# One decode step in a two-layer hybrid decoder: four of the eight rows side by side in TensorE's column groups, without masks, and the second layer's step cut into five pieces between attention units

## The chip, the cores and the metric

The kernel runs on one core of a Trainium2 chip. The metric is the device time of one execution in microseconds (us); lower is better. The engines are named as the profile names them: PE (TensorE matmuls) and PEld (its weight loads), DVE (VectorE), ACT (ScalarE), POOL (GpSimd), SP (SyncE, which issues most of the DMAs).

## The reference, cut to what matters

A 1024-token prompt and eight decode rows (one token each) go through two layers together. Three places handle the eight rows by themselves, since each row has its own cache or state:

```python
def mem_attend(qm, mem_k, mem_v):            # both layers; 4 heads of 64, 256 memory tokens per row
    s = einsum('blhd,bmhd->bhlm', q, mem_k) * MEM_HEAD_DIM ** -0.5
    return einsum('bhlm,bmhd->blhd', softmax(s), mem_v)

def swa_sample(q, k_all, v_all, rel_bias, sinks):    # layer 1; 12 heads on 4 kv heads, 128 cached keys per row
    p = exp(s + bias - m);  p = p / (sum(p) + exp(sink - m));  return p @ v

def gla_chunk_step(S, inp):                  # layer 0; per row and head one 96 x 192 state
    S_new = exp(g) * S + k v^T;  o = q @ S_new
```

Everything else (norms, projections, MLPs, the prompt's own attention) is done for prompt and decode rows in common.

## The kernel before, in words

All operands are fp32. The 1032 columns (1024 prompt tokens, 8 decode rows) are cut into three chunks of 384, 384 and 264. Large projections split each operand into two halves (`split`: a cast on ACT, a subtraction on DVE) and do three matmuls per tile (`proj`, L246 to L248). The order on each engine is fixed when the program is built: a scheduler places the instructions by its own cost model, and each engine then runs its list in order, waiting on semaphores.

The decode work stands in three functions or blocks.

- `mem_attend_dec` (L418), called once per layer. The eight rows share one PSUM tile of 32 partitions (8 rows times 4 heads). For the matmul of row `b` the stationary operand is a 128x32 matrix that is zero outside the four columns of that row, made by multiplying q with a mask from memory (`dmask`, L427) or, for the probabilities, with an identity (`eyeb`, L451). So 16 matmuls (8 rows, 2 halves) of 256 columns accumulate one after another, for scores (L434) and again for values (L459). In layer 0 the keys and values come through SP's queue into 3 buffers; in layer 1 through POOL's queue into 8.
- The gated linear attention's decode block (L1520 to L1543): for each of 4 heads the state `sin` and the broadcast row `vb` are loaded, ACT scales the state (L1534), DVE adds the new outer product (L1535), the new state is stored (L1536), and 8 matmuls of 192 columns (L1539) form the output in 8 partitions. `sin` and `vb` have two buffers each, so head 2 waits for head 0's store.
- `swa_dec` (L1706), in layer 1: the memory step, then the local attention of the eight rows with 96 partitions (12 heads times 8 rows): 16 matmuls of 128 columns (L1735), softmax, one transpose, a masked copy (L1759), 8 matmuls of 256 columns (L1764), transposes back into `q`. It is called as a whole before the unit `(t, i2) = (5, 2)`.

Layer 1's prompt attention consists of 24 units `swa(t, i2)`: a score block on PE (L1657, PSUM tile `sA`), softmax on DVE (L1661, L1682) and ACT (L1676), eight transposes (L1689, `sT`), a copy on ACT (L1691), a value block (L1700, `sf`). Until `t = 4` the projections `in_b` stand between the units; from `(4, 0)` on nothing of that kind is left. `Arena` hands out the memory of layer 1's normalised inputs (`ar` in the profile) to the decode step once `in_b` no longer reads them; the output projection takes the same tiles next.

The class `Row` adds an ordering edge between matmuls so that they keep their order on PE. The prompt attention uses it for matmuls that write PSUM partitions 0 to 63 and 64 to 127 by turns (L413, L1700).

Of the kernel before, what the change touches and what calls it, by code (L numbers as in the profile page):

```python
# [47 lines left out]
def hybrid_decoder_step(ctx: ExitStack, tc: tile.TileContext, A, O):  # L48
# [29 lines left out]

    eyeb = cp.tile([P, NDEC, NDEC], F32, tag="eyeb", name="eyeb")
# [338 lines left out]
    def mem_attend_dec(l, ap, q, psS, psT, psO, bufs=3, dq_=None):  # L418
        dma = dq_ or nc.sync
        dq = q[:, :, SEQ:NT]  # L420
        mk = ap.tile([P, NDEC, 32], F32, tag="dmask", name=nm("dmask"), bufs=1)
        ps = psS()
        qms = []
        for hp in range(2):
            dma.dma_start(mk, A["mem_mask"][hp])
            qm = ap.tile([P, NDEC, NDEC, 4], F32, tag=f"dqm{hp}", name=nm("dqm"), bufs=1)
            TT(qm, mk.rearrange("p a (b c) -> p a b c", c=4),  # L427
               dq[:, hp, :].unsqueeze(1).unsqueeze(3).to_broadcast([P, NDEC, NDEC, 4]), ALU.mult)
            qms.append(qm.rearrange("p a b c -> p a (b c)"))
        for b in range(NDEC):  # L430
            kb = ap.tile([P, 2, MEM], F32, tag="kvb", name=nm("kb"), bufs=bufs)
            dma.dma_start(kb, A["mem_kT"][l, b])
            for hp in range(2):
                nc.tensor.matmul(ps[:32, :MEM], qms[hp][:, b, :], kb[:, hp, :],  # L434
                                 start=(b == 0 and hp == 0), stop=(b == NDEC - 1 and hp == 1))
        mx = small(1, 32, "mx")
        nc.vector.tensor_reduce(mx, ps[:32, :MEM], AX.X, ALU.max, negate=True)
        p = ap.tile([32, MEM], F32, tag="dp", name=nm("dp"), bufs=1)
        sm = small(1, 32, "msum")
        nc.scalar.activation(p, ps[:32, :MEM], AF.Exp, bias=mx, accum_out=sm)  # L440
        rs = small(1, 32, "mrs")
        nc.vector.reciprocal(rs, sm)
        nc.vector.tensor_scalar(p, p, rs, None, ALU.mult)
        tps = psT()
        for mt in range(2):
            nc.tensor.transpose(tps[:, mt * 32 : mt * 32 + 32], p[:, mt * P : (mt + 1) * P], ident[:32, :32])
        pt = ap.tile([P, 2, 32], F32, tag="dpt", name=nm("dpt"), bufs=1)
        nc.vector.tensor_copy(pt.rearrange("p a b -> p (a b)"), tps[:, :64])
        ptm = ap.tile([P, 2, NDEC, 32], F32, tag="dptm", name=nm("dptm"), bufs=1)
        for mt in range(2):  # L450
            TT(ptm[:, mt].rearrange("p a (b c) -> p a b c", c=4),  # L451
               pt[:, mt, :].rearrange("p (b c) -> p b c", c=4).unsqueeze(1).to_broadcast([P, NDEC, NDEC, 4]),
               eyeb.unsqueeze(3).to_broadcast([P, NDEC, NDEC, 4]), ALU.mult)
        po = psO()
        for b in range(NDEC):
            vb = ap.tile([P, 2, MEM], F32, tag="kvb", name=nm("vb"), bufs=bufs)
            dma.dma_start(vb, A["mem_v"][l, b])
            for mt in range(2):
                nc.tensor.matmul(po[:32, :MEM], ptm[:, mt, b, :], vb[:, mt, :],  # L459
                                 start=(b == 0 and mt == 0), stop=(b == NDEC - 1 and mt == 1))  # L460
        od = ap.tile([32, MEM], F32, tag="dp", name=nm("od"), bufs=1)
        nc.vector.tensor_copy(od, po[:32, :MEM])
        ots = psT()
        for hp in range(2):
            nc.tensor.transpose(ots[:, hp * 32 : hp * 32 + 32], od[:, hp * P : (hp + 1) * P], ident[:32, :32])
        otv = ots[:, :64].rearrange("p (a b c) -> p a b c", a=2, c=4)
# [1104 lines left out]
    with ExitStack() as sl1:  # L1571
# [8 lines left out]
        with ExitStack() as sa:  # L1580
# [199 lines left out]
            for t in range(6):  # L1780
                if t < 5:
                    in_b(t)
                if t == 3:
                    in_b(5)
# [151 lines left out]
```

## Time and profile before

| | |
|---|---|
| median of three runs | 2256.66 us (2255.68 to 2261.45) |
| the profiled execution | 2265.92 us, span 2264.1 us |
| PE busy | 2195.5 us, 97% of the span |
| DVE, ACT, POOL busy | 67%, 47%, 3% |
| mean granted TensorE clock | 0.989 of 2.4 GHz |

PE is busy nearly all the time; DVE and ACT have room on the average. In a timeline row the first number is the start, the second the time until the last result of the row is out; matmuls overlap in a pipeline, so the time that a row costs PE is the distance from its start to the start of the row behind it. An fp32 matmul appears as two records.

### The profile page before, as it was taken

What the parts mean: (1) busy time and instruction counts of PE and PEld (TensorE: products, weight loads), DVE (VectorE), ACT (ScalarE), POOL (GpSimd) and SP (SyncE); (2) the same over time, 40 slices, a digit from 0 to 9 for tenths busy, and PEclk for the clock granted to TensorE, in tenths of its full rate; (3) what the DMA queues carried; (4) which work ended last, traced back from release to release, by engine and by line L of the source; (5) the groups of instructions that cost most, each with busy time, mean ns of one, the idle gap of its engine ahead of it and who ended that gap; (6) DMA issues with size and microseconds to landing.
All of it is one profiled execution on the core that took longest, in us unless ns stands there. A gap on an engine that the chain in (4) does not pass through costs nothing. (4 is left out here: it accounts for less than half of the span.)

```text
span 2264.1 us, 40118 instructions
## 1 busy us (share of the span) xinstructions
PE 2195.5 (97%) x16244; PEld 2078.0 (92%) x16244; DVE 1513.7 (67%) x2803; ACT 1061.7 (47%) x2071; POOL 79.0 (3%) x80
## 2 busy tenths in 40 slices
PE   8999999999999999989999999999999999999997
PEld 5868898899999999989999878589999999999996
DVE  6645545847987776857469455646887777756557
ACT  6353434647654444333334355545764445333434
POOL 0001100000000000310000000200000000000000
PEclk9999999999999999999999999999999999999998
DMA  5512015534454438574325201313364445735422
GB/s 182 162 52 85 21 57 128 161 100 142 140 187 155 155 135 323 205 261 142 99 74 152 89 20 36 118 62 116 107 203 152 155 154 209 255 107 160 152 95 75
DMA packets 136370, 304.64 MB, mean 135 GB/s; under 512 B 11273, under 2 KB 65985, under 8 KB 135889
## 3 DMA queue, kind: packets, MB, share of 16 engines
q1 hardware_dynamic: 122928, 275.88, 37.1%
q0 software_dynamic: 3312, 13.30, 1.9%
q10 hardware_dynamic: 9936, 12.81, 1.5%
q8 instruction: 130, 2.13, 0.4%
q14 instruction: 64, 0.52, 0.1%
HBM read 214.50 MB, written 89.51 MB: 134 GB/s over the span
## 5 line engine op out<-in xcount | busy, mean ns | idle before, releaser
L154 ACT CAST wh<-ws 128x512 fp32r<-128x512 f32 (+1 forms) x262 | 188.1, 726 | 332.0 <-DVE ws L580 108.3
L727 PE MATMUL mx<-xf,wh 128*128 128x258 f32 x1048 | 297.7, 284 | 0.0
L728 PE MATMUL mx<-xf,wh 128*128 128x258 f32 x1048 | 296.0, 282 | 0.0
L729 PE MATMUL mx<-xf,wl 128*128 128x258 f32 x1048 | 295.1, 282 | 0.0
L155 DVE TENSOR_TENSOR wl<-ws,wh 128x512 fp32r<-128x512 f32 (+1 forms) x262 | 213.7, 822 | 121.6 <-ACT wh L154 120.7
L246 PE MATMUL mm<-xh,wh 128*128 128x384 f32 (+1 forms) x864 | 282.7, 328 | 3.0 <-issue 2.9
L248 PE MATMUL mm<-xh,wl 128*128 128x384 f32 (+1 forms) x864 | 281.3, 326 | 1.8 <-issue 1.8
L247 PE MATMUL mm<-xl,wh 128*128 128x384 f32 (+1 forms) x864 | 278.7, 323 | 0.0
L154 ACT CAST wh<-wr 128x1024 fp32r<-128x1024 f32 x98 | 103.0, 1051 | 294.0 <-PE sx L893 274.9
L892 PE MATMUL mx<-sa,wh 128*128 128x258 f32 x784 | 222.5, 285 | 8.4 <-DVE acc L560 5.9
L155 DVE TENSOR_TENSOR wl<-wr,wh 128x1024 fp32r<-128x1024 f32 x98 | 124.8, 1274 | 151.0 <-ACT wh L154 151.0
L893 PE MATMUL mx<-sa,wh 128*128 128x258 f32 x784 | 221.3, 283 | 0.3 <-DVE sa L155 0.3
L894 PE MATMUL mx<-sa,wl 128*128 128x258 f32 x784 | 221.1, 282 | 0.0
L728 PEld LDWEIGHTS mx<-xf,wh 128*128 128x128 f32 x1048 | 198.0, 189 | 0.4
L727 PEld LDWEIGHTS mx<-xf,wh 128*128 128x128 f32 x1048 | 197.6, 189 | 0.4
L729 PEld LDWEIGHTS mx<-xf,wl 128*128 128x128 f32 x1048 | 197.9, 189 | 0.0
L246 PEld LDWEIGHTS mm<-xh,wh 128*128 128x128 f32 x864 | 163.9, 190 | 13.4 <-issue 10.1
L248 PEld LDWEIGHTS mm<-xh,wl 128*128 128x128 f32 x864 | 163.6, 189 | 10.1 <-issue 8.1
L247 PEld LDWEIGHTS mm<-xl,wh 128*128 128x128 f32 x864 | 164.0, 190 | 6.0 <-issue 4.8
L892 PEld LDWEIGHTS mx<-sa,wh 128*128 128x128 f32 x784 | 148.2, 189 | 9.2 <-issue 6.1
L893 PEld LDWEIGHTS mx<-sa,wh 128*128 128x128 f32 x784 | 149.2, 190 | 0.6 <-DVE sa L155 0.6
L894 PEld LDWEIGHTS mx<-sa,wl 128*128 128x128 f32 x784 | 148.7, 190 | 0.0
(544 smaller groups left out, 5773.9 us busy)
## 6 DMA issues: line engine op xcount, KB each, us to landing
ra<-awd SPq DMA_DIRECT2D x98, 516.0 KB, 4.1
ws<-in_w_up SPq DMA_DIRECT2D x64, 512.0 KB, 6.1
wr<-in_w_downb SPq DMA_DIRECT2D x56, 512.0 KB, 5.8
awd<-aw SPq DMA_DIRECT2D x26, 1032.0 KB, 7.0
awd<-am SPq DMA_DIRECT2D x28, 774.0 KB, 8.4
ws<-in_w_in_a SPq DMA_DIRECT2D x20, 512.0 KB, 3.8
xd<-f ACTq DMA_DIRECT2D x24, 384.0 KB, 4.7
ws<-in_w_out SPq DMA_DIRECT2D x16, 512.0 KB, 3.6
```

What stands on the lines that cost most here:

```text
L154: nc.scalar.copy(hi, src)
L155: (eng or nc.vector).tensor_tensor(lo, src, f32(hi), ALU.subtract)
L246: nc.tensor.matmul(ps[:M, :n], wh[:, k, :M], xh[:, k, :], start=(k == 0), stop=False)
L247: nc.tensor.matmul(ps[:M, :n], wh[:, k, :M], xl[:, k, :], start=False, stop=False)
L248: mm = nc.tensor.matmul(ps[:M, :n], wl[:, k, :M], xh[:, k, :], start=False, stop=(k == KT - 1))
L727: nc.tensor.matmul(ps, wh(k), xh, start=(k == 0), stop=False)
L728: nc.tensor.matmul(ps, wh(k), xl, start=False, stop=False)
L729: mm = nc.tensor.matmul(ps, wl(k), xh, start=False, stop=(k == n - 1))
L892: nc.tensor.matmul(ps, wh[:, q, ms], h, start=(jj == 0 and q == 0), stop=False)
L893: nc.tensor.matmul(ps, wh[:, q, ms], lo, start=False, stop=False)
L894: mm = nc.tensor.matmul(ps, wl[:, q, ms], h, start=False, stop=end)
```

## The change

Matmuls of four decode rows now write four different groups of 32 PSUM partitions: row `b = 2g + e` uses partitions `32g` to `32g + 31`, and `e` picks the columns inside the group (four per `e` in the memory step, twelve in the local attention, one in the gated one). The stationary matrices are zeroed once by POOL and the columns in use are written by small copies, so masks and identity products are gone. Softmax and transposes work on 128 partitions instead of 32 or 96. `Row` keeps the groups in turn.

In layer 0 the memory step stands ahead of the transposes of the gates' decode part, its 16 loads go through POOL's queue, and it has 8 buffers: the values' loads are issued behind the scores and take the keys' buffers. In layer 1 the memory step and the local step become generators that run in step: `next(dec, None)` ahead of each unit from `(4, 2)` on.

```diff
-    def mem_attend_dec(l, ap, q, psS, psT, psO, bufs=3, dq_=None):
...
+    def mem_dec_steps(l, ap, q, psS, psT, psO, bufs=8, dq_=None):
...
+        qm = ap.tile([P, 2, NDEC, 32], F32, tag="dqm", name=nm("dqm"), bufs=1)
+        nc.gpsimd.memset(qm, 0.0)
         ptm = ap.tile([P, 2, NDEC, 32], F32, tag="dptm", name=nm("dptm"), bufs=1)
+        nc.gpsimd.memset(ptm, 0.0)
         for hp in range(2):
             for j in range(2):
                 rows = slice(64 * j, 64 * j + 64)
+                for e in range(2):
+                    nc.vector.tensor_copy(qm[rows, hp, e::2, 4 * e + 2 * hp + j], dq[rows, hp, e::2])
...
+        def grouped(ps, tiles, w):
+            row = Row()
+            for e in (1, 0):
+                for a in range(2):
+                    for g in (3, 2, 1, 0):
+                        b = 2 * g + e
+                        row(nc.tensor.matmul(ps[32 * g : 32 * g + 32, :MEM], w[:, a, b, :], tiles[b][:, a, :],
+                                             start=(e == 1 and a == 0), stop=(e == 0 and a == 1)))
+
+        keys = load(A["mem_kT"][l])
+        values = load(A["mem_v"][l]) if bufs > NDEC else None
+        yield
+        ps = psS()
+        grouped(ps, keys, qm)
+        values = values or load(A["mem_v"][l])
...
+        yield
+        tps = psT()
+        for mt in range(2):
+            nc.tensor.transpose(tps[:, mt * P : mt * P + P], p[:, mt * P : (mt + 1) * P], ident)
+        tpv = tps[:, : 2 * P].rearrange("p (m g c) -> p m g c", m=2, c=32)
+        for e in range(2):
+            nc.vector.tensor_copy(ptm[:, :, e::2, 4 * e : 4 * e + 4], tpv[:, :, :, 4 * e : 4 * e + 4])
+        yield
+        po = psO()
+        grouped(po, values, ptm)
...
+                with tc.tile_pool(name="md0", bufs=1, reuse_waits="tile") as ap:
+                    mem_attend_dec(0, ap, qm, psS, psT, psO, 8, nc.gpsimd)
                 gps = stps()
...
-                for bb in range(NDEC):
-                    nc.tensor.matmul(ops[:NDEC, :DV], qmk[:, bb, :], sin[:, bb, :],
-                                     start=(bb == 0), stop=(bb == NDEC - 1))
-                nc.vector.tensor_copy(vdec[:, hv], ops[:NDEC, :DV])
+                row = Row()
+                for e in range(2):
+                    for g in range(4):
+                        row(nc.tensor.matmul(ops[32 * g : 32 * g + 32, :DV], qmk[:, h, 2 * g + e, :],
+                                             sin[:, 2 * g + e, :], start=(e == 0), stop=(e == 1)))
...
             def swa_dec():
                 ap = Arena(["xl2", "xh2", "xh1", "xl1", "xh0"])
-                mem_attend_dec(1, ap, qx, stps, stps, stps, 8, nc.gpsimd)
+                mem = mem_dec_steps(1, ap, qx, stps, stps, stps, 8, nc.gpsimd)
+                next(mem)
...
+                yield
+                next(mem)
                 ps = stps()
+                row = Row()
+                for e in range(2):
+                    for pr in range(2):
+                        for g in range(4):
+                            b = 2 * g + e
+                            row(nc.tensor.matmul(ps[32 * g : 32 * g + 32, :P], qmk[:, pr, b, :], kc[:, b, pr, :],
+                                                 start=(e == 0 and pr == 0), stop=(e == 1 and pr == 1)))
...
+                if t == 4:
+                    dec = swa_dec()
                 for i2 in range(NB // 2):
-                    if (t, i2) == (5, 2):
-                        swa_dec()
+                    if (t, i2) >= (4, 2):
+                        next(dec, None)
                     swa(t, i2)
```

What this does to the order on PE is seen at three places. In layer 0 the value matmuls of the memory step (`vb` or `kb` the loaded values, `mm` the projection of the GLA's q and k, `xh`, `xl` its inputs) stand on PE in the program before in these rows:

```order
L247 MATMUL mm_1746<-xl_128,wh_1742 128x384
L459 MATMUL sf_1413<-vb_1414,dptm_1410 32x256 x2
L459 MATMUL sf_1413<-vb_1418,dptm_1410 32x256 x2
L459 MATMUL sf_1413<-vb_1422,dptm_1410 32x256 x2
L248 MATMUL mm_1746<-xh_127,wl_1743 128x384
L246 MATMUL mm_1746<-xh_127,wh_1742 128x384
```

In the changed program PE has, in their place:

```order
L450 MATMUL sf_1412<-kb_1397,dptm_1340 32x256
L450 MATMUL sf_1412<-kb_1393,dptm_1340 32x256
L450 MATMUL sf_1412<-kb_1389,dptm_1340 32x256
L450 MATMUL sf_1412<-kb_1385,dptm_1340 32x256
...
L450 MATMUL sf_1412<-kb_1395,dptm_1340 32x256
L450 MATMUL sf_1412<-kb_1391,dptm_1340 32x256
L450 MATMUL sf_1412<-kb_1387,dptm_1340 32x256
L450 MATMUL sf_1412<-kb_1383,dptm_1340 32x256
...
L482 MATMUL sT_1431<-ident,od_1429 128x128 x2
```

The sixteen stand in one block, and its first matmul reads `kb_1397`, the last of the eight value loads. Between the end of the scores and this block PE has 28 projection matmuls of 384 columns and 24 of 264.

In the gated linear attention (`sin` the state, `ot` transposes of the prompt's output, `mm`, `mx` the gate projection), PE's rows at the last two heads before:

```order
L1539 MATMUL sx_5286<-sin_5263,qmk_5267 8x192 x6
L246 MATMUL mm_5488<-xh_191,wh_5364 128x384
L1539 MATMUL sx_5286<-sin_5263,qmk_5267 8x192 x2
...
L248 MATMUL mm_5488<-xh_191,wl_5365 128x384
L1557 MATMUL ot_5760<-ident,vtok 128x128
L1539 MATMUL sf_5319<-sin_5296,qmk_5300 8x192 x8
L1557 MATMUL ot_5760<-ident,vtok 128x128 x2
```

And in the changed program:

```order
L246 MATMUL mm_5490<-xh_190,wl_5367 128x384
L1578 MATMUL ot_5762<-ident,vtok 128x128 x3
L1578 MATMUL ot_5771<-ident,vtok 128x128 x3
L1578 MATMUL ot_5780<-ident,vtok 128x128 x3
L1578 MATMUL ot_5789<-ident,vtok 128x128 x3
L1560 MATMUL sx_5288<-sin_5265,qmk 32x192 x8
L1560 MATMUL sf_5321<-sin_5298,qmk 32x192 x8
L1578 MATMUL ot_5798<-ident,vtok 128x128 x3
L244 MATMUL mx_5526<-xh_190,wh_5372 128x384
```

The matmuls of heads 2 and 3 moved behind the whole projection `mm` and four groups of transposes.

In layer 1 (units: `sA` scores, `sT` transposes, `sf<-pt` values; decode: operands `ar`), PE's last rows of the attention before:

```order
L459 MATMUL sx_16630<-ar_16583,ar_16585 32x256 x4
L459 MATMUL sx_16630<-ar_16584,ar_16585 32x256 x8
...
L1689 MATMUL sT_16818<-ident,z_16793 128x128 x6
L1735 MATMUL sf_16675<-ar_16586,ar_16585 96x128 x8
L1689 MATMUL sT_16818<-ident,z_16793 128x128 x2
L1755 MATMUL sx_16726<-ident,ar_16586 128x96
L1764 MATMUL sf_16730<-ar_16587,ar_16586 96x256 x8
L1770 MATMUL sx_16740<-ident,ar_16587 128x96 x2
L1700 MATMUL sf_16783<-pt_16781,vtok_14255 64x128 x8
L246 MATMUL mm_16911<-xh_16900,wh_16854 128x384
```

In the changed program (the last two groups here are those of units (5, 1) and (5, 3), and `mm_16912` is the output projection):

```order
L1722 MATMUL sf_16487<-pt_16485,vtok_14257 64x128 x8
L1679 MATMUL sA_16616<-kf,q 128x128
L1770 MATMUL sf_16529<-ar_16406,ar_16407 32x128 x16
L1679 MATMUL sA_16616<-kf,q 128x128
...
L1788 MATMUL sx_16609<-ident,ar_16408 128x128
...
L1799 MATMUL sf_16674<-ar_16407 32x256 x8
...
L1722 MATMUL sf_16720<-pt_16718,vtok_14257 64x128 x8
L1679 MATMUL sA_16796<-kf,q 128x256 x2
L482 MATMUL sf_16730<-ident,ar_16408 128x128 x2
L1679 MATMUL sA_16796<-kf,q 128x256 x2
L244 MATMUL mm_16912<-xh_16901,wh_16855 128x384
```

The decode step's chain of transpose, values and transposes, which stood together ahead of the output projection, now has whole units between its pieces; the transposes and values of units (5, 2) and (5, 3) moved behind the first output-projection matmul.

## Rows read from the trace of the kernel before

**Rows 1.** The page's first part: busy time, share of the span and instructions of each engine.

```profile
PE 2195.5 (97%) x16244; PEld 2078.0 (92%) x16244; DVE 1513.7 (67%) x2803; ACT 1061.7 (47%) x2071; POOL 79.0 (3%) x80
```

**Rows 2.** Busy time of the engines in two stretches: the gated block, and layer 1 from the last `in_b` matmul to the first matmul of the output projection. Columns: stretch, its length, then PE, PEld, DVE, ACT, POOL busy (instructions), granted clock, DMA share, GB/s.

```profile
378.80:404.70 25.90, 25.57 (x136) 16.34 (x136) 14.14 (x41) 11.21 (x33) 0.00 (x0) 1.00 0.83 211
1425.00:1492.10 67.10, 57.73 (x392) 36.67 (x390) 39.84 (x154) 34.44 (x102) 12.10 (x23) 0.90 0.28 87
```

**Rows 3.** The decode matmuls of layer 0, grouped by line and shape over the whole span: records | busy, mean ns of one | idle before.

```profile
L434 PE MATMUL sA<-kb,dqm 128*32 128x256 f32 x32 | 7.8, 382 | 0.1
L459 PE MATMUL sf<-vb,dptm 128*32 128x256 f32 x32 | 7.5, 382 | 0.8 <-DMA vb<-in_mem_v 0.8
L1539 PE MATMUL sx<-sin,qmk 96*8 96x192 f32 x32 | 6.4, 327 | 0.5 <-DVE sin L1535 0.5
L1539 PE MATMUL sf<-sin,qmk 96*8 96x192 f32 x32 | 5.7, 327 | 0.3 <-DVE sin L1535 0.3
```

**Rows 4.** PE in order of time: a block of 24 records of the masked form in layer 1 and what stands behind it; and in layer 0 a block of the prompt's value matmuls, which write partitions 0 to 63 and 64 to 127 by turns, and what stands behind that.

```profile
1466.08 5.37 PE L459 MATMUL sx<-ar,ar 128*32 128x256 f32 x24
1471.28 1.89 PE L459 MATMUL sx<-ar 128*32 128x256 f32 x8
...
157.51 1.08 PE L413 MATMUL sf<-pt,vtok 128*64 128x256 f32 x8
158.53 0.44 PE L248 MATMUL mm<-xh,wl 128*128 128x384 f32 x1
```

**Rows 5.** Weight loads of 32 and of 128 columns: least/median/greatest ns.

```profile
L434 PEld LDWEIGHTS sA<-kb,dqm x32: 106/110/110, 162.0 to 174.1; 128*32 128x32 f32 x32
L727 PEld LDWEIGHTS mx<-xf,wh x1048: 187/188/193, 576.9 to 1914.2; 128*128 128x128 f32 x175
```

**Rows 6.** POOL's queue in layer 1: the eight key loads as POOL issues them (busy, mean ns of one), and the time of such a load from issue to landing; the same of a load in SP's queue in layer 0; PE in layer 0 at the first and the 22nd of a run of projection matmuls (21 of 384 columns lie between these two starts) and the one behind; and the minimum over the gates on DVE.

```profile
L432 POOL DMA_DIRECT2D ar<-in_mem_kT x8 | 4.2, 538 | 0.0
...
ar<-in_mem_kT POOLq DMA_DIRECT2D x8, 256.0 KB, 4.8
...
kb<-in_mem_kT SPq DMA_DIRECT2D x8, 256.0 KB, 2.8
...
174.85 0.34 PE L246 MATMUL mm<-xh,wh 128*128 128x384 f32 x1
...
178.50 0.28 PE L246 MATMUL mm<-xh,wh 128*128 128x264 f32 x1
178.62 0.28 PE L247 MATMUL mm<-xl,wh 128*128 128x264 f32 x1
...
175.02 3.33 DVE L1307 TENSOR_REDUCE sm<-vtok 128x8 f32<-128x3072 f32 x1
```

**Rows 7.** The gated block's heads 2 and 3 in order of time: the loads on SP's queue, head 3's state on DVE, and PE behind it; last the landing time of the `vb` loads (L1530).

```profile
387.81 6.17 SPq L1528 DMA_DIRECT2D sin<-in_state_gla  x2
394.03 0.53 SPq L1530 DMA_DIRECT2D vb<-vdd  x1
...
401.50 2.72 DVE L1535 SCALAR_TENSOR_TENSOR sin<-vb,qd,sin 96x192 f32<-96x192 f32 x8 [1.18 <-ACT sin L1534]
...
404.70 0.76 PE L1557 MATMUL ot<-ident,vtok 128*128 128x128 f32 x5
...
409.08 0.45 PE L246 MATMUL mx<-xh,wh 128*128 128x384 f32 x1 [2.29 <-DVE t L1230]
...
DMA to landing us min/median/max: 6.2/6.9/7.6
```

**Rows 8.** PE in layer 1: a value block, a transpose block and a score block of prompt units with the starts of what stands behind them; and the end of the decode step with the output projection behind it.

```profile
1425.92 1.09 PE L1700 MATMUL sf<-pt,vtok 128*64 128x128 f32 x16
1426.95 1.09 PE L1689 MATMUL sT<-ident,z 128*128 128x128 f32 x8
1427.97 0.70 PE L1657 MATMUL sA<-kf,q 64*128 64x256 f32 x2
...
1430.22 1.13 PE L1657 MATMUL sA<-kf,q 64*128 64x256 f32 x8
1431.29 0.62 PE L434 MATMUL sx<-ar 128*32 128x256 f32 x2
...
1484.03 6.16 PE L1764 MATMUL sf<-ar,ar 128*96 128x256 f32 x16 [1.34 <-DVE ar L1759]
...
1492.05 0.44 PE L246 MATMUL mm<-xh,wh 128*128 128x384 f32 x1
```

**Rows 9.** PE's busy time and granted clock in two parts of that stretch. Columns: stretch, length, PE busy (records), clock, DMA share, GB/s.

```profile
1431.90:1441.50 9.60, 7.82 (x33) 0.64 0.56 196
1479.40:1491.00 11.60, 7.31 (x23) 0.71 0.00 1
```

**Rows 10.** DVE's masked products in the same stretch, and the DMA rate at its start: group | busy, mean ns | idle before; then length, PE, PEld, DVE, ACT, POOL busy, clock, DMA share, GB/s.

```profile
L1731 DVE TENSOR_TENSOR ar<-ar,q 128x48 f32<-128x48 f32 x16 | 2.8, 202 | 2.4 <-DMA ar<-in_swa_mask 2.2 <-PE sf L1735 0.2
L1759 DVE TENSOR_TENSOR ar<-ar,eyeb 128x768 f32<-128x768 f32 x1 | 1.0, 958 | 0.0
L427 DVE TENSOR_TENSOR ar<-ar,qx 128x256 f32<-128x256 f32 x2 | 0.8, 424 | 0.2 <-DMA ar<-in_mem_mask 0.2
L451 DVE TENSOR_TENSOR ar<-ar,eyeb 128x256 f32<-128x256 f32 x2 | 0.8, 420 | 0.0
...
1425.00:1435.00 10.00, 7.69 (x67) 4.91 (x65) 7.51 (x27) 5.48 (x15) 6.92 (x13) 0.97 0.92 292
```

## What the change should do to the time

> **What bounds the kernel now.** The page comes first: PE is busy for 97% of the span [rows 1], so nearly everywhere the time is PE's own and a matmul taken away is time won. The three decode places are the ones to test, so I read the busy times of the stretches that hold them, then PE in order of time there. In layer 0 the masked matmuls run without a gap but for 0.8 us at the values [rows 3]. In the gated block PE shows only 0.3 us free out of 25.9 [rows 2], but the DMA share there is 0.83, and head 3 comes at the end of a chain of transfers that has nothing to do with PE [rows 7]. The layer-1 stretch is different: of 67.1 us PE works 57.7, and its mean granted clock is 0.90 [rows 2]. In two parts of it the clock is 0.64 and 0.71, a mixture of the levels 2.4 and 1.2 GHz, and in both PE stands idle for part of the time, 1.8 us of 9.6 and 4.3 of 11.6 [rows 9]. The last of these is the local step's chain at the end, where 16 value records take 6.16 us [rows 8].
>
> **The price of a masked and of a grouped record.** Twenty-four masked records take 5.20 us from start to start, 0.217 each [rows 4]. A memory step has 64 of them, 13.9 us. No row shows four column groups. The nearest form is the prompt's value block, which writes two halves of the partitions by turns: 8 records take 1.02 us [rows 4], that is four rounds of 0.217 plus 0.15; one after another they would take 1.74. So two groups run side by side, and I take four to do so as well: 32 records make eight rounds, 8 x 0.217 + 0.15 = 1.9 us a set, 3.8 a step. If only two overlapped it would be 3.6 a set, if none 6.9. Weight loads stand against it if four of them took longer than one round. A load of 32 columns shows 110 ns and one of 128 shows 188 [rows 5], so 96 more columns cost 78 ns, 0.8 a column; four loads of 32 at that rate take some 105 ns, half a round. They don't bind.
>
> A rule speaks against small blocks: the Trainium skill, "TensorEngine Tiling (Array Packing)", section "Key Properties", says that changing the tiling mode drains the engine. The 0.15 us of the prompt's block would hold such a drain, and no row shows it apart. By the row ten lone blocks would cost 1.5 us in all; the rule gives no figure.
>
> **Layer 0's memory step.** PE loses 13.9 us of matmuls and the wait of 0.8 and gets 3.8: 10.9 won. Against that stand new waits. The value loads now wait for the scores, since they take the keys' buffers, and go through POOL: eight issues of 0.54 us, then 4.8 us from issue to landing [rows 6], so the last is there 4.3 + 4.8 = 9.1 us after the scores. The first value matmul reads just that one. Ahead of it PE has 28 matmuls of 384 columns and 24 of 264, at (178.50 - 174.85)/21 = 0.174 and 0.12 us [rows 6], with small transposes some 8.2 us: 0.9 of wait. On DVE the copies of the probabilities can stand behind the minimum over the gates, 3.33 us [rows 6], and a split; I allow 0.5, and 0.5 more for the gates' own chain, whose transposes are later now. An earlier value load would win these back, and if the copies lose another place the set stands still for up to 4 us more. So **-9**, between -5 and -11.
>
> **The gated block.** 64 records are 12.1 us busy [rows 3] and become some 5.7 with the groups: 6 us fewer by PE alone. But head 3's state can't be loaded until the store of head 1 has freed its buffer; the load of `vb` behind it is issued at 394.03, takes 0.5 to issue and 6.9 to land, so it is there near 401.4, and DVE's product starts at 401.50 and ends at 404.2 [rows 7]. None of that gets faster. PE goes on with the value of head 3 at about 404 at the earliest, and then waits for DVE's release of `mx` at 409.08 as before [rows 7]. What PE saves in heads 0 and 1 it stands still ahead of head 2. **-0.5**, between -5.7 (the loads start earlier by as much as PE runs ahead) and +1.5 (ten lone blocks of 0.15, above).
>
> **Layer 1.** Taken out: 64 masked records, the local step's masked ones, and DVE's masked products, 5.4 us [rows 10]. Put in: two sets of 1.9, a local score set of half that and a value set of 1.0, and 24 small copies of about 0.17 on DVE, 4.1 us. Moved: the five pieces, now with a unit between each, so that softmax and copies lie behind other PE work; and three blocks of the last units, 1.02 to 1.03 each [rows 8], which go behind the first output-projection matmul. From the last `in_b` matmul to that one PE then has 8 score blocks of 1.06, 7 transpose blocks of 1.02, 8 value blocks of 1.03 [rows 8] and some 8 us of decode work: 32 us. DVE has 39.8 [rows 2] - 5.4 + 4.1 less two replaced copies of 0.25, near 38. How near can the stretch come to that? *One end*: DVE dense, 38. *Other end*: PE's 32, plus all of today's idle time (67.1 - 57.7 = 9.4), plus all that today's clock costs (0.10 x 67.1 = 6.7): 48. In both the three blocks come back behind it (3.1) and the tail has no unit left to hide its last wait (1.5, the size of the 1.34 now [rows 8]). That gives 67.1 - 38 - 4.6 = 24.5 and 67.1 - 48 - 4.6 = 14.5. I take 43, the middle, since idle time goes with the chain at the end but a unit's own chain stays: **-19.5**.
>
> The memset and the loads on POOL lie beside other work: 16 loads of layer 1 ran there before, in a stretch in which 292 GB/s moved [rows 10].
>
> **Sum**: 9 + 0.5 + 19.5 = 29. The profiled execution took 2265.9, 9.3 above the median; it should become 2237. The sum is a difference, so against the median it is 2256.7 - 29 = **2228**.
>
> **Rivals.**
> 1. *The gated block pays too.* Its loads on SP's queue start earlier because the buffers come free earlier. For it: PE reads each state in a fraction of the time. Against: the buffer is freed by the store, not by PE [rows 7]. Another 5.2: 2222.5.
> 2. *Layer 1 runs dense.* The stretch ends at DVE's 38: 5 more, 2223. Against: waits of score, softmax, copy within a unit stay.
> 3. *Only two groups overlap at a time.* 3.6 a set: 3.4 more per memory step and about 1.7 for the local sets, 2236. Against: nothing but that no row shows four.
> 4. *The clock stays at half in layer 1.* PE's share is smaller now and has a wait in every unit; 32 us become 64, and the gain of the stretch is gone: 2256.7 - 9.5, 2247. For it: the two parts with 0.64 and 0.71 [rows 9]. Against: the clock over the whole was 0.90 with 14% idle [rows 2]. The Trainium skill, "TensorE: Matmul & The Clock Gate", section "HAM oscillation — how this bites in real kernels", describes a kernel whose short bursts with waits between them are throttled again at each; by it this rival would hold. The low rows of the clock agree with it for bursts, the mean over the stretch doesn't.
> 5. *No overlap at all*, and masks were beside the point: 6.9 a set. Layer 0 then loses a microsecond or two, layer 1 gains about 8 from the cut alone: 2250, no change to speak of.
> 6. *Slower*: POOL's queue moves its 256 KB loads one after another, in t us each. Four sets of eight hang on it, with cover of 8.2 us for layer 0's values (above) and, counted the same way, 11.6, 10.6 and 10 for the others: 32t - 40.4. It eats the 29 from t = 2.2. At the 2.8 that one load in SP's queue takes [rows 6] it is 49: 2277. Against: eight issued 0.54 apart that land in 4.8 each are through 8.6 us after the first, 1.1 each [rows 6].
>
> **Chances.** Forecast 0.50 (2223 to 2233 by itself); rival 1: 0.12; 2: 0.12; 3: 0.08; 4: 0.10; 5: 0.05; 6: 0.03. 0.3%, 6.8 us, is about what a measurement of this kernel can tell from no change; only rival 5 lies within it and only 6 beyond, so faster 0.92, same 0.05, slower 0.03. The range leaves out rivals 4 to 6: up to 2240, where the bounds of layer 1 (5 more) and layer 0 (4 more) meet, and down to 2215, where rivals 1 and 2 come together.
>
> **What would show it.** The blocks of 32 records should take 1.9 us start to start, where two groups make 3.6. PE should wait about a microsecond before layer 0's values for a POOL load, and several before the gated block's heads 2 and 3 for DVE's state product. The layer-1 stretch should be 43 us long with no clock below 0.9. I'm wrong if the blocks take other times, if PE doesn't wait in the gated block, or if that stretch is outside 38 to 48.

## The result and the profile after

| | before | after |
|---|---|---|
| median of eight runs | 2259.6 us (2255.3 to 2267.0) | 2239.0 us (2231.1 to 2251.1) |
| the profiled execution | 2265.92 us, span 2264.1 us | 2243.39 us, span 2241.6 us |
| PE busy | 2195.5 us | 2165.5 us |
| mean granted TensorE clock | 0.989 | 0.987 |

The ratio is 0.9913 (95% interval 0.9895 to 0.9930): 19.7 us faster, 16 to 24 by the interval. The forecast was 29 faster; 2239 lies at the upper edge of its range, and the gain is two thirds of the forecast. The first part of the page after, which answers to [rows 1]:

```profile
PE 2165.5 (97%) x16250; PEld 2062.8 (92%) x16250; DVE 1505.1 (67%) x2811; ACT 1060.2 (47%) x2071; POOL 90.0 (4%) x99
```

Most of PE's list is the same in both programs, so one can look up when the same matmul starts in either trace. Six such matmuls cut the program into stages. The differences of their starts, in us:

| stage | before | after | change |
|---|---|---|---|
| start to the memory step of layer 0 | 158.5 | 158.1 | -0.4 |
| layer 0's memory step, to the first decay block of the gated attention | 44.3 | 32.4 | **-12.0** |
| the prompt's gated attention | 161.6 | 161.9 | +0.2 |
| gated decode block and its output projection | 101.0 | 103.5 | **+2.5** |
| from there to layer 1's last `in_b` matmul (code that no edit touches) | 959.2 | 957.8 | -1.5 |
| layer 1 from there to one of PE's last matmuls, 13 us ahead of the end in both | 826.6 | 815.1 | **-11.6** |

So layer 0 gave 3 us more than forecast (-9), the gated block cost 3 more (-0.5), and layer 1 gave 8 less (-19.5).

**Layer 0.** PE in order of time after (start, time until the last result, records, the wait ahead in brackets), then POOL's issues of the value loads and the time from issue to landing:

```profile
168.90 1.50 PE L450 MATMUL sA<-kb,dqm 128*32 128x256 f32 x24 [0.71 <-DMA kb<-in_mem_kT]
170.33 0.91 PE L1294 MATMUL sf<-vtok 128*128 128x384 f32 x2
...
181.07 1.93 PE L450 MATMUL sf<-kb,dptm 128*32 128x256 f32 x32
182.94 0.44 PE L244 MATMUL mm<-xh,wh 128*128 128x384 f32 x1
...
170.22 4.25 POOL L440 DMA_DIRECT2D kb<-in_mem_v  x8 [8.85 <-PE sA L450]
...
kb<-in_mem_v POOLq DMA_DIRECT2D x8, 256.0 KB, 4.8
```

The 32 value records take 182.94 - 181.07 = 1.87 us, the forecast 1.9: four groups run side by side. There is no wait ahead of them. The loads are issued from 170.22 on, before the scores end near 172.3, since the first half of the records frees four of the buffers; the last is issued at 173.9 and, by the median of 4.8 us from issue to landing, there near 179.3 (an estimate).

**The gated block.** PE around heads 2 and 3 after, and busy times and clock of the same piece (columns as in [rows 2]):

```profile
386.59 2.82 PE L1560 MATMUL sx<-sin,qmk 96*32 96x192 f32 x16 [0.45 <-DVE sin L1554]
390.17 3.46 PE L1560 MATMUL sf<-sin,qmk 96*32 96x192 f32 x16 [0.77 <-DVE sin L1554]
394.64 0.87 PE L1578 MATMUL ot<-ident,vtok 128*128 128x128 f32 x3 [1.01 <-DVE sr L1582]
397.67 0.69 PE L244 MATMUL mx<-xh,wh 128*128 128x384 f32 x1 [2.15 <-DVE t L1247]
398.15 0.52 PE L245 MATMUL mx<-xl,wh 128*128 128x384 f32 x1
398.47 0.52 PE L246 MATMUL mx<-xh,wl 128*128 128x384 f32 x1
...
383.90:397.60 13.70, 8.19 (x49) 3.42 (x47) 11.07 (x34) 8.03 (x25) 0.00 (x0) 0.80 0.58 137
```

PE works 8.2 of 13.7 us there. It waits 0.45 and 0.77 us for DVE's state products ahead of the two heads, and inside them it keeps DVE's pace: eight products take 2.71 us a head. Rows of DVE and ACT after, then DVE's of head 2 before:

```profile
384.51 1.02 DVE L1582 TENSOR_TENSOR sr<-ot,sr 128x384 f32<-128x384 f32 x2 [2.67 <-PE ot L1578]
386.12 2.71 DVE L1554 SCALAR_TENSOR_TENSOR sin<-vb,qd,sin 96x192 f32<-96x192 f32 x8
389.71 2.71 DVE L1554 SCALAR_TENSOR_TENSOR sin<-vb,qd,sin 96x192 f32<-96x192 f32 x8
...
385.10 0.51 ACT L152 CAST xh<-sr 128x384 fp32r<-128x384 f32 x1 [4.25 <-DVE sr L1582]
385.52 5.63 ACT L1553 ACTIVATE sin<-sin,eg 96x192 f32<-96x192 f32 x16
```

```profile
395.96 2.71 DVE L1535 SCALAR_TENSOR_TENSOR sin<-vb,qd,sin 96x192 f32<-96x192 f32 x8
```

Neither ACT's scaling nor DVE's products wait for a load after. Both stand in their engine's list behind work on `sr`, and that waits 2.67 us on DVE, 4.25 on ACT, for transposes that PE has behind the whole projection `mm`. Counted from the stage's start, head 2's products begin at 33.8 us (386.12 - 352.32), before at 31.5 (395.96 - 364.50). This is read from the lists; no run changes their order alone.

The matmuls of 384 columns behind the block start 0.32 us apart instead of 0.17: the clock is at 1.2 GHz. It is full through head 2, falls at the end of head 3 and stays low for 10.2 us. Before, it was full through the block [rows 2], but fell in the same projection for some 3.5 us. Two stretches after, one before:

```profile
386.50:389.50 3.00, 2.38 (x16) 0.71 (x16) 2.39 (x9) 3.00 (x10) 0.00 (x0) 1.00 0.26 75
392.10:402.30 10.20, 6.99 (x27) 5.69 (x28) 7.28 (x23) 4.22 (x12) 0.00 (x0) 0.50 0.23 62
```

```profile
410.40:413.90 3.50, 3.50 (x13) 3.50 (x13) 2.35 (x9) 2.95 (x7) 0.00 (x0) 0.51 0.00 0
```

So the +2.5 us have three parts. The projection starts 45.4 us after the stage's start instead of 44.6: 0.8. Its nineteenth matmul comes 5.35 us after its first instead of 4.80, which is the clock: 0.6. The rest, 1.1, comes behind that, where PE's waits for DVE are 2.8 us instead of 0.4 (sum, times, longest; two rows after, one before):

```profile
PE mx L245 <- DVE xl L153: 1.4, 1, 1.4
PE ot L1578 <- DVE sr L1582: 1.4, 2, 0.9
```

```profile
PE mx L247 <- DVE xl L155: 0.4, 2, 0.3
```

**Layer 1.** From the last `in_b` matmul (counted from the last but one, 0.12 us ahead) to the output projection's second tile (the point from which both programs have the same list): before, with its longest waits (sum, times, longest), and after, with its waits and the stretch in which the clock is low:

```profile
1424.73:1498.32 73.59, 64.04 (x437) 42.40 (x436) 46.33 (x160) 40.80 (x111) 12.10 (x23) 0.91 0.26 81
...
PE sx L1755 <- DVE ar L1753: 2.4, 1, 2.4
PE sf L1700 <- ACT pt L1691: 2.0, 3, 1.2
PE sA L1657 <- DVE sm L1661: 1.8, 1, 1.8
PE sf L1764 <- DVE ar L1759: 1.3, 1, 1.3
```

```profile
1413.59:1476.62 63.03, 50.33 (x435) 33.66 (x434) 44.16 (x162) 39.34 (x109) 10.56 (x21) 0.89 0.31 98
...
PE sT L1711 <- DVE z L1704: 4.2, 4, 1.6
PE sf L1722 <- ACT pt L1713: 3.2, 5, 1.2
PE sA L1679 <- DVE sm L1683: 2.3, 3, 1.8
PE sT L1711 <- DVE sm L1781: 2.0, 1, 2.0
...
1420.70:1434.00 13.30, 11.19 (x63) 6.42 (x66) 8.35 (x36) 6.25 (x24) 1.10 (x2) 0.62 0.46 160
...
1462.00 0.44 PE L244 MATMUL mm<-xh,wh 128*128 128x384 f32 x1 [0.55 <-ACT xh L152]
```

PE's busy time fell by 13.7 us, its idle time rose from 9.6 to 12.7, and the clock did not rise. Before, 4.5 us of the waits stood ahead of the decode step's matmuls (`ar`; the two rows and 0.8 more) and 4.8 ahead of the units'. After, 0.4 stands ahead of the step's and 11.7 ahead of the units': transposes for DVE's normalised `z`, values for ACT's copy, scores for a score tile that DVE still reads. The output projection starts 48.4 us after the last `in_b` matmul (1413.59 to 1462.00), but reaches its second tile 14.6 us later, where it took 6.3 before.

### The profile page after: what moved, and what is told of

It reads as the page before. It is cut to its first block, busy times and chain, and to the rows that moved or that the text cites. A ratio compares the mean times of both kernels' runs of the same rounds, so it can differ in the third digit from the quotient of the medians.

```text
span 2241.6 us, 40146 instructions
## 1 busy us (share of the span) xinstructions
PE 2165.5 (97%) x16250; PEld 2062.8 (92%) x16250; DVE 1505.1 (67%) x2811; ACT 1060.2 (47%) x2071; POOL 90.0 (4%) x99
## 4 chain that ended last, share of the span: by engine, by line
PE 77%; DMA 6%; DVE 5%; ACT 2%; POOL 1%; issue 1%; SPq 0%; DVEq 0%; ACTq 0%; POOLq 0%
PE mm L244 5%; PE mx L745 5%; PE mx L746 5%; PE mm L246 5%; PE mx L747 5%; PE mm L245 5%; PE mx L910 3%; PE mx L912 3%; PE mx L911 3%; PE mm L745 2%; PE mm L746 2%; PE mm L747 2%; PE mx L244 2%; PE mx L246 2%; PE mx L245 2%; PE mm L910 2%
## 5 line engine op out<-in xcount | busy, mean ns | idle before, releaser
L153 DVE TENSOR_TENSOR sa<-ra,sa 128x1032 fp32r<-128x1032 f32 x98 | 125.7, 1282 | 35.1 <-ACT sa L152 35.1
```

The source lines that it names most:

```text
L153: (eng or nc.vector).tensor_tensor(lo, src, f32(hi), ALU.subtract)
```

## Experiments

All are edits of the changed kernel. Stage times are from the traces, one execution of each, as above; the ratio is that of the timed runs to the kernel before, with its 95% interval. How far programs differ in a stretch that they share can be read too: layer 1's stretch to the second tile took 63.0 us in the changed kernel and 63.8 to 63.9 in the three runs that leave layer 1 as it is.

**Groups without turns.** The same matmuls of the memory steps, one group after another.

```diff
-            for e in (1, 0):
-                for a in range(2):
-                    for g in (3, 2, 1, 0):
+            for g in (3, 2, 1, 0):
+                for e in (1, 0):
+                    for a in range(2):
```

> The changed kernel with the memory step's matmuls (both layers) ordered group by group, so that eight records in a row write the same 32 partitions; same matmuls, same stationary matrices. Theory of overlap: a set of 32 records then takes 32 x 0.217 = 6.9 us instead of 1.9, so layer 0 ends 8 to 10 us later and layer 1 loses up to 10, less where PE waited anyway. Rival (the masks' removal and the moves are what counted): no stretch changes by more than 2 us.

Layer 0's stage took 37.7 us (32.4 with the turns), layer 1 818.5 (815.1); ratio 0.9955 (0.9939 to 0.9972). The overlap matters, but a set took not 6.9 us but 4.5:

```profile
185.15 4.59 PE L450 MATMUL sf<-kb,dptm 128*32 128x256 f32 x32
189.68 0.44 PE L244 MATMUL mm<-xh,wh 128*128 128x384 f32 x1
...
185.61 0.59 PE L450 MATMUL sf<-kb,dptm 128*32 128x256 f32 x2
...
186.26 0.62 PE L450 MATMUL sf<-kb,dptm 128*32 128x256 f32 x4
...
189.15 0.59 PE L450 MATMUL sf<-kb,dptm 128*32 128x256 f32 x2
```

The last three rows are what is under way in short windows at the begin, in the middle and at the end of the block: four records in the middle, two at either end (in the middle of the changed kernel's block, at 182.4, eight). Single records start at 185.15, .39, .61 and .83, from 186.04 on they start in pairs: the matmuls of the next group begin while four records of the one ahead are still to run. Four alone, twelve pairs, four alone make 20 rounds of 0.22, 4.4 us. So even this order overlaps by two, and my price for no overlap at all was not reached.

**Layer 0's step as before**: masks, SP's queue, three buffers, its old place behind the flag of the gates.

```diff
-                    mem_attend_dec(0, ap, qm, psS, psT, psO, 8, nc.gpsimd)
+                    mem_dec_old(0, ap, qm, psS, psT, psO)
```

> The changed kernel with layer 0's memory step as before (masks, loads through SP's queue, three buffers, at its old place); gated block and layer 1 as changed. If the 12.1 us between the traces at layer 0 belong to this step, the gated decay's first block starts 11 to 13 us later than in the changed kernel. Rival: 2 us or more of them are chance of the one execution, or belong to an effect of other edits on the loads: 8 to 10 us later.

The stage took 43.3 us against 32.4, 10.9 more: at the lower edge of the first expectation. The step as a whole (groups, queue, buffers and place together) gives 11 to 12 us; of this the turns alone give 5.3, by the run before. Ratio 0.9962 (0.9941 to 0.9983).

**The gated block masked as before.**

```diff
-                for e in range(2):
-                    for g in range(4):
-                        row(nc.tensor.matmul(ops[32 * g : 32 * g + 32, :DV], qmk[:, h, 2 * g + e, :],
-                                             sin[:, 2 * g + e, :], start=(e == 0), stop=(e == 1)))
+                for bb in range(NDEC):
+                    nc.tensor.matmul(ops[:NDEC, :DV], qmk[:, bb, :], sin[:, bb, :],
+                                     start=(bb == 0), stop=(bb == NDEC - 1))
...
```

> The changed kernel with the gated block's decode matmuls as before (masked, 8 partitions), all else as changed. First theory: the groups made the gated block worse, since its heads 2 and 3 wait for their state however fast PE is, and PE stood still and then ran at half clock (in the changed kernel's trace the block ends 2.5 us later against its own start than before): this kernel is 2 to 3 us faster than the changed one, and PE waits less than 1.5 us in that block. Rival: the block was late for another reason (layer 0's earlier end shifted its transfers): the block takes as long as in the changed kernel, within 0.7 us.

The block's stage took 99.6 us, against 103.5 in the changed kernel; the piece around heads 2 and 3 (380 to 394) has PE 11.4 us busy of 14 at full clock:

```profile
380.00:394.00 14.00, 11.38 (x65) 6.87 (x65) 10.96 (x32) 8.00 (x25) 0.00 (x0) 1.00 0.74 180
```

In the ten traces with the groups the stage took 102.5 to 104.9 and in the four with masks (the kernel before is one) 99.6 to 101.0, so the groups cost 1.5 to 5 us here, some 3 in the middle. PE's waits up to the projection's first matmul fell from 4.7 to 3.1 us, not below 1.5 as I expected; those behind it fell from 2.8 to 0.6, head 2's products begin at 31.5 us again, ahead of the work on `sr`, and the half clock is gone from the whole stage. How much each of these gives is not separated. In the timed runs it doesn't show: 0.9916 (0.9890 to 0.9941).

**Four buffers for the gated states** (`sin` and `vb`).

```diff
-                sin = dp.tile([DK, NDEC, DV], F32, tag="sin", name=nm("sin"))
+                sin = dp.tile([DK, NDEC, DV], F32, tag="sin", name=nm("sin"), bufs=4)
...
```

> The changed kernel with four buffers instead of two for the states and the broadcast rows of the gated block, so that no load waits for a store. First theory: the chain from head 1's store to head 3's state is what PE waits for: without it the block gets 5 to 8 us shorter than in the changed kernel (some 6 us of matmuls plus the half clock behind the wait). Rival: the loads themselves, at a DMA share of 0.82, set the state's time: less than 2 us shorter.

Neither: the stage took 104.9 us, a little longer. SP's queue in that run:

```profile
366.37 0.43 SPq L1547 DMA_DIRECT2D sin<-in_state_gla  x1
369.37 5.11 SPq L1555 DMA_DIRECT2D out_sg_sample<-sin  x2
374.54 0.53 SPq L1549 DMA_DIRECT2D vb<-vdd  x1
```

Head 2's state is loaded early now, but its `vb` load still stands behind both stores in SP's list, and these wait for DVE's products. In this run the loads do bind: DVE waits 1.5 us for `vb` ahead of head 2's products and 1.6 ahead of head 3's. The projection starts 1.3 us earlier in the stage than in the changed kernel, and what stands behind it takes 2.7 more. So the order of the queue sets these loads, not the buffers alone. Ratio 0.9931 (0.9911 to 0.9950).

**Layer 1's step in one piece**, before unit (5, 2).

```diff
-                if t == 4:
-                    dec = swa_dec()
...
-                    if (t, i2) >= (4, 2):
-                        next(dec, None)
+                    if (t, i2) == (5, 2):
+                        for _ in swa_dec():
+                            pass
```

> The changed kernel with layer 1's step not cut: as a whole before unit (5, 2), as it stood before, but with the groups. First theory: most of layer 1's 10.6 us came from PE's saved matmuls and little from the cut, so the distance from the last in_b matmul to the output projection's second tile stays within 3 us of the changed kernel's 62.6. Rival: the cut is what won, and without it that distance is 68 us or more.

The stretch took 61.3 us, 1.7 less than with the cut; layer 1 to the end 814.9 against 815.1. The cut won nothing that the trace shows. The timed runs lean the other way: ratio 0.9939 (0.9917 to 0.9961) against 0.9913 (0.9895 to 0.9930) with the cut. The intervals overlap, and the trace is of the fastest of this kernel's five executions, so whether the cut is worth some us stays open.

**Layer 1 without the step.**

```diff
-                mem = mem_dec_steps(1, ap, qx, stps, stps, stps, 8, nc.gpsimd)
...
-                next(mem)
-                ps = stps()
...
```

> The changed kernel with layer 1's decode step left out (memory and local attention of the eight rows with their loads; only the stores of the caches stay), so the eight rows keep their queries as outputs. What is left of the stretch is the prompt units' own chain. Theory: the units bound the stretch now, and the step costs little above them: the stretch from the last in_b matmul to the second tile of the output projection stays above 52 us (62.6 in the changed kernel, 73.2 before), though PE's records of the step, some 9 us, are gone. Rival: PE's work is the bound as at the start: the stretch falls by all that the step has on PE, 12 us or more with its waits, to 50 or less.

```profile
1412.50:1466.30 53.80, 44.55 (x317) 32.43 (x316) 34.37 (x118) 35.40 (x102) 0.31 (x1) 0.81 0.03 11
...
PE sA L1679 <- DVE sm L1683: 4.3, 3, 1.9
PE sT L1711 <- DVE z L1704: 3.1, 2, 1.5
PE sf L1722 <- ACT pt L1713: 1.6, 4, 0.6
```

53.8 us are left when the whole step is gone, with 9.2 us of idle time and the clock at 0.81: by the number the first theory. But the step isn't hidden under the units: it costs 9.2 us here (63.0 - 53.8), about as much as its records on PE; of before's 73.6 it was 19.8. My forecast for this stretch, 73.6 - 19.5 = 54.1, was as long as it is without the step: it gave the step away for nothing. Nor are the 53.8 the units' chain alone, since the clock is lower here than with the step (0.89). Ratio 0.9885 (0.9866 to 0.9905).

**Filling PE's wait.** Fourteen transposes of the identity ahead of the score block of unit (4, 2).

```diff
+                if (t, i2) == (4, 2):
+                    for _ in range(14):
+                        row(nc.tensor.transpose(spare[0][:, 256:384], ident, ident))
...
+                spare.append(kps)
```

> The changed kernel with 14 transposes of the identity, written to unused columns and never read, ordered on PE just ahead of the score block at which PE waits 1.8 us in layer 1; the rest of the order is unchanged but for one matmul. They take about 1.8 us, so the wait is filled. Theory of the clock: it is this wait after which PE runs at half clock for 11 us, and with the wait filled the clock stays at 1.00 from there to the value loads; layer 1 gets 3 to 6 us shorter. Rival (the units' own chain of DVE and ACT is the bound there, the half clock is hidden under it): the clock stays up, but the stretch changes by less than 1.5 us. Second rival: the clock falls as before.

```profile
1416.45 1.75 PE L1677 MATMUL sx<-ident 128*128 128x128 f32 x14
1418.30 0.59 PE L450 MATMUL sx<-ar,ar 128*32 128x256 f32 x2
...
1417.00:1430.00 13.00, 11.87 (x108) 7.61 (x107) 9.80 (x43) 8.21 (x29) 3.73 (x7) 1.00 0.56 204
```

The wait is filled and the clock stays at 1.00. At the scores of the memory step the run is 2.2 us further ahead of the changed kernel than it was before the fill, at the second tile 1.7: the stretch took 61.3 us, between the theory and its rival. Ratio 0.9912 (0.9878 to 0.9945).

**Filling four more waits** (ahead of the transposes of units (4, 3), (5, 0), (5, 2), (5, 3)).

```diff
+                for _ in range({(4, 3): 14, (5, 0): 8, (5, 2): 12, (5, 3): 8}.get((t, i2), 0)):
+                    row(nc.tensor.transpose(tps[:, 3 * P : 4 * P], ident, ident))
```

> The changed kernel with filling transposes of the identity, never read, ahead of the score block of unit (4, 2) as in the first fill and also ahead of the transposes of units (4, 3), (5, 0), (5, 2) and (5, 3), 14, 14, 8, 12 and 8 of them. Theory of the clock: with the waits filled the granted clock over the layer-1 stretch goes from 0.89 to 0.97 or more, and the stretch from 63.0 to 57 us or less, since the clock costs 0.11 x 63 = 6.9. Rival (the units' chain of DVE and ACT ends the waits): the clock rises, PE waits the less at work and the longer for the chain, and the stretch stays at 60 to 63.

The stretch took 64.6 us at a mean clock of 0.89, PE busy for 56.6: longer, and the clock no better. The theory of the clock falls in this form. The order on PE also changed (the output projection's first matmul comes 58.8 us after the stretch's start instead of 48.4), so that the run doesn't price the fill alone. Ratio 0.9913 (0.9884 to 0.9943).

**Small copies on POOL.**

```diff
-                            nc.vector.tensor_copy(qmk[rows, pr, e::2, c : c + 5 : 2],
+                            nc.gpsimd.tensor_copy(qmk[rows, pr, e::2, c : c + 5 : 2],
...
```

The eight copies of the memory step (`qm`) are moved in the same way.

> The changed kernel with layer 1's 16 small copies of q into the zeroed operands on POOL instead of DVE. Theory: they stand in DVE's list between a unit's maxima, where DVE is busy 7.4 of 9.2 us, and cost PE part of the 1.8 us wait; DVE is rid of 16 x 0.08 to 0.13 us there, the wait shrinks by about 0.7 us and layer 1 by 0.7 to 2. Rival: DVE waits for ACT's exponentials at that place in any case, no change beyond 0.5 us; or POOL's copies are late behind its loads and the scores wait: 1 to 3 us longer.

The stretch took 61.1 us. But not as expected: the wait at the score block stayed the same, and yet the clock behind it was full:

```profile
1414.63 1.13 PE L1679 MATMUL sA<-kf,q 64*128 64x256 f32 x6 [1.78 <-DVE sm L1683]
...
1417.00:1430.00 13.00, 11.37 (x140) 7.39 (x138) 8.06 (x32) 9.33 (x30) 5.21 (x13) 1.00 0.53 167
```

In the changed kernel a wait of 1.79 us at that place is followed by 0.62. So this wait alone doesn't decide over the clock; what does stays open, and that the fill kept it up in the run above is not shown either. At the scores of the memory step this run, too, is 2.2 us ahead of the changed kernel: that is what the half clock costs there. Ratio 0.9915 (0.9889 to 0.9941).

**A projection later**, to put PE work beside the units.

```diff
-                if t == 3:
-                    in_b(5)
                 if t == 4:
+                    in_b(5)
                     dec = swa_dec()
```

> The changed kernel with the projection in_b(5) called ahead of the units t = 4 instead of t = 3, so that its 72 matmuls stand later. Theory: what layer 1 lacks after the last in_b is PE work beside the units' chains, so the idle time there (12.7 us from the last in_b matmul to the second tile of the output projection, and the half clock) shrinks when in_b ends later: layer 1 gets 3 to 8 us shorter. Rival: the decode step's loads need the memory that in_b frees, so the step comes later by as much and the tail takes the gain back: within 2 us, or up to 5 us longer.

From a common matmul ahead of it to the end the program got 1.3 us longer than the changed one: within the rival's 2 us. Programs with the same layer 1 differ there by as much (up to 1.3), so longer is not shown. The later step met the same chain of units with fewer units left; that this gave the gain back was not tried. Ratio 0.9914 (0.9881 to 0.9946).

**Together**: block masked, first fill, copies on POOL.

> The changed kernel with three edits together: the gated block masked as before, the 14 filling transposes in layer 1, and layer 1's small copies on POOL. By the single runs' traces the block gives 4 to 5 us and layer 1 some 1.5 to 3.5: 6 to 8 us less than the changed kernel in the trace's stretches, a ratio to before of 0.988 to 0.990. Rival: the gains in layer 1 are given back by the half clock at its tail, as the fill alone showed in part: 4 to 5 us less, 0.989 to 0.991.

The block's stage took 101.0 us, layer 1 811.7: 5.9 us less than the changed kernel in the two. Timed, 0.9902 (0.9884 to 0.9919), median 2235.3: the lowest of the complete kernels, but its interval holds the changed kernel's 0.9913, so better is not shown. With the four further fills:

> The same with the gated block masked as before and layer 1's small copies on POOL. Clock theory: 10 to 12 us less than the changed kernel in the trace's stretches (4 to 5 in the block, 6 to 7 in layer 1), ratio to before 0.986 to 0.988. Rival: 6 to 7 us less, 0.988 to 0.990, as without the further fills.

0.9915 (0.9893 to 0.9937); the block's stage 100.7 us, layer 1 814.5: the fills took back what the copies and the first fill gave.

## Why the prediction was right or wrong

- **The total** lies in the range partly by luck: layer 0 gave 3 us more than its term. With 9 from there the median would have been near 2242, beyond the 2240.
- **Four groups side by side: right**, 1.87 us a set. Rivals 3 and 5 fall, and with no value load late and 0.7 us at the first keys rival 6 as well.
- **Layer 0: right in kind, 3 us too small** (-9 against -12, and -10.9 by the step put back). Of the 1.9 us for new waits only 0.7 came, and at the first keys, which I had not named. None came at the values, because their loads start while the scores still run; I had counted them from the last score. And the masked sets cost 15.0 us, not 13.9 (start of each piece to the start of the row behind it): they stood in seven pieces.
- **The gated block: the path was wrong** (-0.5, at worst +1.5; measured +2.5, and 1.5 to 5 by the masked traces). PE did stop for DVE's product before heads 2 and 3, 0.45 and 0.77 us instead of the several that I named. But I had it from the chain of store and loads, and in the changed kernel no product waits for a load. The products stand in DVE's list behind work that waits for PE's moved transposes. I had read that move in PE's order and had not followed it to DVE. Two terms are missing: the waits for DVE behind the projection's start (2.8 us instead of 0.4) and the clock (0.6 us in the projection); I had priced half clock in layer 1 only. My 5.7 us for the 64 grouped records was worked out from no row: priced like the memory sets they are 16 x 0.171 + 4 x 0.15 = 3.3 us (0.171 from (404.70 - 401.97) / 16 before, an estimate), but PE isn't the bound there.
- **Layer 1: the term that failed** (-19.5 against -10.6 to the second tile). PE's saving in busy time, 13.7 us, is there, and the waits ahead of the decode step's matmuls fell from 4.5 us to 0.4, as the step "I take 43, the middle, since idle time goes with the chain at the end" has it. But that step put the units' waits below today's idle time, and they rose from 4.8 to 11.7 us; the lost clock stayed. I wrote that a unit's own chain "stays" and gave it no size. Without any decode step 9.2 us of idle time are left, and 53.8 us in all, what I had forecast with the step in it. The stretch to the output projection took 48.4, just outside my bounds of 38 to 48, with the clock at 0.89, below my 0.9; and 8.3 instead of 4.6 came back behind it. How the 53.8 divide into the units' chain and half clock stays open: priced as I priced the clock, 0.19 x 53.8 = 10 us of them would be the clock (an estimate).
- **Rival 4, half clock**, came in part: 0.89 after, 0.91 before. The fill and the copies on POOL, both with full clock behind the first wait, gained 1.7 and 1.9 us; filling five waits gained nothing.
- **Rival 1** (the block pays too) and **rival 2** (layer 1 dense) are refuted by the two stages.

The Trainium skill's "HAM oscillation — how this bites in real kernels", in "TensorE: Matmul & The Clock Gate", had bursts with waits between them throttled again and again. Layer 1's low stretch agrees in kind (0.62 behind a wait of 1.79 us), though the waits in the Trainium skill's kernel are longer; the run with the copies on POOL, full clock behind the same wait, shows that a single wait doesn't tell.

## What to carry to other kernels

Matmuls with few output columns are worth putting in column groups where PE is the bound: 32 records in 1.9 us instead of 6.9. Where another chain ends the wait, first find the time of the stretch without the work in question, here 53.8 us; the work came on top of it with about its own time on PE, 9.2 us. Follow a moved block into the lists of the other engines: what waits for it there holds up whatever stands behind it. And price a new wait with the clock behind it: behind a wait of 1.8 us in layer 1 the half clock cost 2.2.

## What the runs showed beyond that

- Matmuls to another column group start while four records of the group ahead are still to run: even group by group, 32 records take 4.5 us.
- The stage between the two layers' decode steps, which no edit touches, differs from program to program by up to 8 us (816.8 to 824.6 us from the gated block's end to a common matmul early in layer 1). Most of it is one wait on DVE of the first MLP, which some programs have and others don't; first row of the changed kernel, second row what the run with four buffers has in that place:

```profile
PE mx L910 <- DVE acc L578: 5.7, 1, 5.7
```

```profile
PE mx L911 <- DVE sa L153: 1.2, 1, 1.2
```

The kernel before has that wait too, 5.9 us, so it is not part of the difference between the two traces. Edits worth less than 8 us can't be ordered by the traces' totals, and the stages are compared instead. Why that wait comes and goes was not tried.
